# Values of two strided head groups made from neighbouring tokens, and attention steps moved by one slot

## The chip, the cores and the metric

The kernel runs on one core of one Trainium2 chip, in one launch. The time is the device time of one execution in microseconds (us), as the median of three runs. TensorE (PE) multiplies matrices, VectorE (DVE), ScalarE (ACT) and GpSimd (POOL) work on elements, SyncE (SP) issues most DMAs. Each of them takes its instructions in the order in which they were written and stops at one whose input is not there.

## The reference

One decoder block in float32, batch 1, 1024 tokens, width 1024. After a first layer norm, `p = h @ W_in` gives the input of a state-space mixer (SSM), then q, k and v of 12 heads of width 64, and two gates. The heads are three groups of four. Group 0 looks back over 128 neighbouring tokens. In group 1 a query sees only every 4th token and in group 2 every 16th, so these two work on strided subsequences:

```
q, k, v = the slices of p;  q, k = rope_partial(q), rope_partial(k)
for gi, (win, dil) in enumerate(((128, 1), (512, 4), (2048, 16))):
    o_g, lse_g = dilated_window_attention(q[group], k[group], v[group], win, dil)
att = softmax over the three groups of lse, times o
mixed = sigmoid(g_ssm) * GLU(gelu(S5(u))) + sigmoid(g_att) * (att @ W_up)
```

The mixture, memory cross-attention and a feed-forward layer follow, each with a layer norm.

## The kernel before

Every large product is done with three PE products: both factors are split into a rounded high part (made on ACT) and a remainder (made on DVE), and high·high, high·low and low·high are added in PSUM (`mm3`, lines L100 to L102). Weights come through a stream `W`: SP loads a block `wraw`, ACT casts it to `whi` (L136), DVE subtracts to `wlo` (L137). Six split blocks may be held; the stream moves by one block in each *slot*.

A slot is the unit of the order, which is written out by hand: some products, then one attention step, then `slot()`, which moves the weight stream and gives one tick to each generator in `sides`. From 290 to 675 us `qkv_pair` runs for three groups and, in each, for four pairs of token tiles (128 tokens a tile). A pair has six slots: four with the q and k products (12 matmuls of 512 columns each), two with the v products (24 matmuls of 256 columns each). The token tile is the stationary operand (`lhsT`); in groups 1 and 2 it is read with a stride of 4 or 8 tokens (`o.sl`). After the fourth slot `rope` (L906 to L917, DVE) takes q and k out of PSUM and rotates them. After the sixth, L947 adds the bias to v.

The attention of a pair a, b runs beside the products of the next slots. `att_T` (L954) transposes q and k, which needs `rope` to be done. `att_S` multiplies them (L969), takes the masked maximum on DVE (L973, L975) and the exponentials on ACT (L977). `att_PT` (L987) transposes the probabilities. `att_PV` (L995, L996) multiplies them with v, and SP writes the result to `at_dr` (L998). Before, T(a) stands in slot 4 and T(b), S(a) in slot 5 of their own pair (slots are counted from 0); PT(a), S(b) in slot 0, PV(a) in 1, PT(b) in 2 and PV(b) in 3 of the next.

The generator `ssm_side` works through twelve blocks, one in six ticks after four idle ones. Tick 0 of a block is `ssm_pe1` (PE L803, L809; ACT, then DVE L375 fill `dts`), tick 2 is `ssm_pe2` (PE L822, then the DVE chain L826 to L838), tick 5 is `ssm_pe3` (PE L845, L846; DVE `yo`). POOL makes the tables of the next block (L733); `ec` and `es` wait for L837 of this one. With six slots in a pair, `ssm_pe2` always stands in slot 0, behind S(b).

After the last pair come 16 half gates with 32 slots. When the attention's rest and the SSM are done, `launch_merge` starts `merge_side`, whose 23 steps make the input of the next product (L1202 and on), the last of them `yh` and `yl` (L1111, L1112).

Of the kernel before, what the change touches and what calls it, by code (L numbers as in the profile page):

```python
# [10 lines left out]
FT = mybir.dt.float32  # L11
# [8 lines left out]
SEQ = 1024  # L20
D = 1024
NT = SEQ // 128
KB = D // 128
# [35 lines left out]
def block_kernel(ctx, tc, I, out, dbg=None):  # L59
# [33 lines left out]
    def mmbank(shape=(128, 512)):  # L93
        return ps.tile(list(shape), FT, name="mm", tag="mm", bufs=4)
# [6 lines left out]
        pe.matmul(o, lhsT=lh, rhs=rl, start=False, stop=False)  # L101
        pe.matmul(o, lhsT=ll, rhs=rh, start=False, stop=last)  # L102

# [1 line left out]
    class Stream:  # L105
        def __init__(self):
            self.req = []
# [55 lines left out]
    W = Stream()  # L163
# [3 lines left out]
    y_dr = dr.tile([G * 16, 8, 128], FT, name="y_dr")  # L167
    h_dr = dr.tile([NT, 128, D], FT, name="h_dr")
    at_dr = dr.tile([3, SEQ, 264], FT, name="at_dr")
    g_dr = dr.tile([16, 128, SEQ], FT, name="g_dr")  # L170

    for nm, n in (("wxk", 8), ("wu", 6), ("wxv", 8)):
# [4 lines left out]
    for j in range(NG4):  # L177
        W.add(I["wg"][j], 1024, ("wg", j))
        for half in range(2):
            sched4.append(("wg", j, half))  # L180
            n = 2 * j + half
            for key in ab_units[16 * n // (2 * NG4):16 * (n + 1) // (2 * NG4)]:
                sched4.append(key)
                W.add(I[key[0]][key[1]], 1024, key)
    W.nstart = len(W.req)
    for g in range(3):
        for i in range(4):
            W.add(I["wqk"][g, i], 1024)
        for i in range(2):
            W.add(I["wv"][g, i], 1024)  # L190
    for i in range(NG4, 16):
        W.add(I["wg"][i], 1024, ("wg", i))
    for m in range(8):
# [12 lines left out]
        for i in range(4):  # L206
            W.add(I["wff2"][4 * hc + i], 1024)

# [1 line left out]
    stp = con  # L210

    def ln_rstd(sts, e, extra=None):
# [68 lines left out]
                if next(g, "end") == "end":  # L281
                    sides.remove(g)

# [1 line left out]
    kv_c, kvp = open_pool("kv", "left")  # L285
    mem_c, memp = open_pool("memp", "left")
    st_c, stl = open_pool("start", "right")
# [53 lines left out]
        transpose_in(x, hh, hl, t)  # L341
        act.dma_start(h_dr[t], x)

# [1 line left out]
    T = {}  # L345

    def load_bq(g):
# [364 lines left out]
    load_bq(1)  # L712
    par_c, parp = open_pool("par", "right")
    sides.append(params(parp))
# [1 line left out]
    ssm_d = None  # L716

    def start_ssm():
# [164 lines left out]
            ds[b].clear()  # L883
            yield

# [1 line left out]
    att_c, att = open_pool("att", "right")  # L887

    def tok(g, n):
# [29 lines left out]
    def qkv_pair(os_, bias, step):  # L919
        last = os_[0].n == 6  # L920
        ps_ = [mmbank() for _ in os_]
        for i in range(4):
            w = [t.rearrange("p (k c) -> p k c", k=2) for t in W.get(0 if last else i)]
            for o, p in zip(os_, ps_):
                for k in (2 * i, 2 * i + 1):
                    mm3(p, hh[:, k, o.sl], hl[:, k, o.sl], w[0][:, k % 2, :], w[1][:, k % 2, :], k == 0, k == KB - 1)
            if last:
                W.done()
            step(i)
            if i == 3:  # L930
                for o, p in zip(os_, ps_):
                    rope(o, p, bias)
            slot()
        ps_ = [mmbank() for _ in os_]
        for i in range(2):
            w = [t.rearrange("p (k c) -> p k c", k=4) for t in W.get(0 if last else 4 + i)]
            for o, p in zip(os_, ps_):
                for k in range(4 * i, 4 * i + 4):
                    mm3(p[:, :256], hh[:, k, o.sl], hl[:, k, o.sl], w[0][:, k % 4, :], w[1][:, k % 4, :], k == 0,
                        k == KB - 1)  # L940
            if last:
                W.done()
            step(4 + i)
            if i == 1:
                for o, p in zip(os_, ps_):
                    o.v = att.tile([128, 256], FT, name="v", tag="v", bufs=4)
                    dve.tensor_add(o.v, p[:, :256], bias[:, 512:768])  # L947
            slot()

    def att_T(o):  # L950
        p = axbank((128, 4, 128))
# [51 lines left out]
    def steps_old(i):  # L1003
# [7 lines left out]
        elif i == 3:  # L1011
            att_PV(hist[-1], hist[-2])

    for g in range(3):
        if g == 1:
            load_bq(2)
        for n in range(0, 8, 2):
            os_ = [new_tile(g, n), new_tile(g, n + 1)]

            def step(i):  # L1020
                if i < 4:
                    if hist:
                        steps_old(i)
                elif i == 4:
                    att_T(os_[0])
                else:
                    att_T(os_[1])
                    att_S(os_[0], hist[-1] if hist else None)

            qkv_pair(os_, T["bq", g], step)  # L1030
            hist += os_

    def att_tail():
        for i in range(4):
            steps_old(i)
            yield

    sides.insert(0, att_tail())

# [1 line left out]
    state = {"att": att_c, "ssm": ssm_c}  # L1041

    def merge_side():
# [128 lines left out]
    close_pool(state["mg"])  # L1172
    ath, atl, yh, yl = (state[k] for k in ("ath", "atl", "yh", "yl"))

# [1 line left out]
    mx_c, mx = open_pool("mx", "right")  # L1176
    xh = actp.tile([128, KB, SEQ], FR, name="acth", tag="acth")
    xl = actp.tile([128, KB, SEQ], FR, name="actl", tag="actl")
# [41 lines left out]
    close_pool(mx_c)  # L1220
    close_pool(state["yf"])

# [1 line left out]
    nat_c, nat = open_pool("nat", "left")  # L1224
    hn = nat.tile([128, NT, D], FT, name="hn")

# [52 lines left out]

    nat_gemm(xh, xl, evac_mix)  # L1280

# [1 line left out]
    ptp_c, ptp = open_pool("ptp", "right")  # L1283
    ph = ptp.tile([128, 4, SEQ], FR, name="ph")
    pl = ptp.tile([128, 4, SEQ], FR, name="pl")
# [44 lines left out]

    nat_gemm(Cat(ph, xh), Cat(pl, xl), evac_xo)

# [1 line left out]
    fh, fl = ph, pl  # L1334
    for t in range(NT):
        defer(t, lambda t=t: dve.scalar_tensor_tensor(hn[:, t, :], hn[:, t, :], ALPHA, bf2, op0=OP.mult, op1=OP.add))
# [74 lines left out]
def _layout(inputs):  # L1411
# [8 lines left out]
    def natblk(w):  # L1420
        k, n = w.shape
        return c(w.reshape(k // 256, 2, 128, n // 512, 512).transpose(3, 0, 2, 1, 4).reshape(-1, 128, 1024))
# [10 lines left out]
    for k, s in (("ln_in_g", A["ln_in_g"]), ("ln_in_b", A["ln_in_b"]), ("b_mix", A["b_mix_out"][0]),  # L1433
# [13 lines left out]
    o["wu"] = colblk(w_in[:, U:Q])  # L1447
    o["wqk"] = np.stack([natblk(np.concatenate([w_in[:, s + 256 * g:s + 256 * g + 256] for s in (Q, K_)], 1))
                         for g in range(3)])
    o["wv"] = c(np.stack([w_in[:, V + 256 * g:V + 256 * g + 256].reshape(2, 4, 128, 256).transpose(0, 2, 1, 3)  # L1450
                          .reshape(2, 128, 1024) for g in range(3)]))
    o["wg"] = colblk(w_in[:, GS:])
    o["wglu"] = colblk(A["w_glu"][0])
    o["wup"] = colblk(A["w_att_up"][0])
# [39 lines left out]
```

## Time and profile before

| | |
|---|---|
| three runs | 1943.19, 1945.00, 1945.46 us, median 1945.0 |
| span of the profiled execution | 1943.7 us, 1.3 under the median |
| PE busy | 1885.0 us, 97% of the span |
| PE's share of the chain that ended last | 86%, three times 26% of it in L100 to L102 |
| DVE, ACT, POOL busy | 966.7 (50%), 563.7 (29%), 609.0 (31%) us |
| mean granted PE clock | 0.990 |
| DMA | 163.26 MB, mean 84 GB/s |

Only the span is given for the profiled execution; the run's own time around it is not shown, and the timed median stands for it. The span leaves out what lies before its first and after its last instruction. A matmul's duration in the trace is that of its way through the array; what a row of them costs is the distance from one start to the next.

### The profile page before, as it was taken

The page shows a single profiled execution, that of the slowest core. Times are in us where ns is not written, and L with a number is a line of the kernel's source. Part 1 is how long each engine was busy: PE and PEld are TensorE (multiplying, and loading weights), DVE is VectorE, ACT ScalarE, POOL GpSimd, SP SyncE. Part 2 cuts the span into 40 slices and gives each one's busy share as a digit, 9 for nine tenths or more (in the row PEclk, how much of TensorE's full clock was granted, in tenths as well). Part 3 has the DMA queues.
Part 4 walks back from the last instruction along what each step waited for, and adds up shares of the span by engine and source line. Part 5 has one row for each costly group of instructions (what it writes and reads, how often), then busy time and mean ns, then how long its engine had stood idle before and what let it go on. Part 6 is the DMA issues. An engine that isn't in the chain of part 4 may idle for free.

```text
span 1943.7 us, 24170 instructions
## 1 busy us (share of the span) xinstructions
PE 1885.0 (97%) x9400; PEld 1619.6 (83%) x9400; DVE 966.7 (50%) x1678; ACT 563.7 (29%) x998; POOL 609.0 (31%) x782
## 2 busy tenths in 40 slices
PE   7899999999999998999999999999999999999996
PEld 7798788889999976788888888788888888888885
DVE  6526846675666666444556445542323223232328
ACT  4324343433332434322124322412121212213121
POOL 3305687474565335322034004401010100101016
PEclk9999999999999999999999999999999999999998
DMA  6545562130120243333511121111111111011102
GB/s 243 184 122 187 183 198 73 34 99 23 55 67 29 75 136 109 118 117 109 185 44 44 44 76 44 44 65 44 55 54 44 44 44 66 32 55 48 62 21 87
DMA packets 82563, 163.26 MB, mean 84 GB/s; under 512 B 19857, under 2 KB 39441, under 8 KB 82449
## 3 DMA queue, kind: packets, MB, share of 16 engines
q1 hardware_dynamic: 75968, 147.30, 22.8%
q10 hardware_dynamic: 5904, 12.85, 1.7%
q0 software_dynamic: 576, 1.57, 0.3%
q8 instruction: 74, 1.21, 0.3%
q14 instruction: 41, 0.33, 0.1%
HBM read 126.99 MB, written 34.70 MB: 83 GB/s over the span
## 4 chain that ended last, share of the span: by engine, by line
PE 86%; DVE 7%; ACT 2%; issue 2%; POOL 2%; DMA 1%; DVEq 0%; SPq 0%; ACTq 0%; POOLq 0%
PE mm L100 26%; PE mm L102 26%; PE mm L101 26%; PE ax L262 1%; DVE wlo L137 1%; PE ax L996 1%; PE ax L969 1%; PE ax L987 1%; PE ax L822 1%; ACT yh L1111 1%; PE ax L845 1%; PE ax L954 1%; PE ax L809 1%; DVE lnst L237 0%; PE ax L846 0%
## 5 line engine op out<-in xcount | busy, mean ns | idle before, releaser
L100 PE MATMUL mm<-acth,whi 128*128 128x512 f32 (+1 forms) x896 | 348.0, 388 | 4.9 <-ACT abst L611 4.6
L102 PE MATMUL mm<-acth,wlo 128*128 128x512 f32 (+1 forms) x896 | 345.5, 386 | 2.5 <-DVE wlo L137 2.5
L101 PE MATMUL mm<-actl,whi 128*128 128x512 f32 (+1 forms) x896 | 345.4, 386 | 0.3 <-DVE actl L256 0.3
L136 ACT CAST whi<-wraw 128x1024 fp32r<-128x1024 f32 (+1 forms) x169 | 168.4, 996 | 419.5 <-PE mm L102 300.9
L137 DVE TENSOR_TENSOR wlo<-wraw,whi 128x1024 fp32r<-128x1024 f32 (+1 forms) x169 | 213.2, 1263 | 146.9 <-ACT whi L136 144.6
L100 PE MATMUL mm<-whi,acth 128*128 128x512 f32 (+1 forms) x704 | 281.7, 400 | 0.0
L102 PE MATMUL mm<-whi,actl 128*128 128x512 f32 (+1 forms) x704 | 270.7, 384 | 0.0
L101 PE MATMUL mm<-wlo,acth 128*128 128x512 f32 (+1 forms) x704 | 270.4, 384 | 0.0
L1350 POOL TENSOR_TENSOR sg<-sg 128x512 f32<-128x512 f32 x64 | 67.8, 1059 | 574.4 <-ACT sg L1349 574.4
L100 PE MATMUL mm<-whi,ph 128*128 128x512 f32 x576 | 224.3, 389 | 0.0
L102 PE MATMUL mm<-whi,pl 128*128 128x512 f32 x576 | 224.1, 389 | 0.0
L101 PE MATMUL mm<-wlo,ph 128*128 128x512 f32 x576 | 224.1, 389 | 0.0
L100 PEld LDWEIGHTS mm<-acth,whi 128*128 128x128 f32 x896 | 171.1, 191 | 38.4 <-ACT abst L611 5.5
L102 PEld LDWEIGHTS mm<-acth,wlo 128*128 128x128 f32 x896 | 170.6, 190 | 36.4 <-DVE wlo L137 3.0
L101 PEld LDWEIGHTS mm<-actl,whi 128*128 128x128 f32 x896 | 171.1, 191 | 32.6 <-DVE actl L256 0.5
L102 PEld LDWEIGHTS mm<-whi,actl 128*128 128x128 f32 x704 | 168.0, 239 | 15.3
L101 PEld LDWEIGHTS mm<-wlo,acth 128*128 128x128 f32 x704 | 168.6, 239 | 14.2
L100 PEld LDWEIGHTS mm<-whi,acth 128*128 128x128 f32 x704 | 167.5, 238 | 15.4
L1352 DVE TENSOR_TENSOR pl<-sg,ph 128x512 fp32r<-128x512 f32 x64 | 44.3, 692 | 261.8 <-ACT ph L1351 261.8
L1368 DVE TENSOR_TENSOR hn<-hn,mm 128x512 f32<-128x512 f32 x128 | 87.0, 685 | 163.7 <-PE mm L102 163.7
L102 PEld LDWEIGHTS mm<-whi,pl 128*128 128x128 f32 x576 | 108.1, 188 | 22.4
L101 PEld LDWEIGHTS mm<-wlo,ph 128*128 128x128 f32 x576 | 108.1, 188 | 22.4
(322 smaller groups left out, 2882.6 us busy)
## 6 DMA issues: line engine op xcount, KB each, us to landing
wraw<-in_wff_dram SPq DMA_DIRECT2D x64, 512.0 KB
wraw<-in_wg_dram SPq DMA_DIRECT2D x16, 512.0 KB
gl<-g_dr SPq DMA_DIRECT2D x32, 256.0 KB
wraw<-in_wqk_dram SPq DMA_DIRECT2D x12, 512.0 KB
wraw<-in_wglu_dram SPq DMA_DIRECT2D x16, 384.0 KB
g_dr<-abst SPq DMA_DIRECT2D x16, 256.0 KB
a_dr<-abst ACTq DMA_DIRECT2D x16, 256.0 KB
b_dr<-abst ACTq DMA_DIRECT2D x16, 256.0 KB
```

Of the source, the lines that this page charges most:

```text
L100: pe.matmul(o, lhsT=lh, rhs=rh, start=first, stop=False)
L101: pe.matmul(o, lhsT=lh, rhs=rl, start=False, stop=False)
L102: pe.matmul(o, lhsT=ll, rhs=rh, start=False, stop=last)
L136: act.copy(h[:, :n], r[:, :n])
L137: dve.tensor_sub(l[:, :n], r[:, :n], h[:, :n].bitcast(FT))
L262: pe.transpose(p[:, k, :], x[:, (4 * b + k) * 128:(4 * b + k + 1) * 128], ident)
L809: pe.matmul(p[:, g, :], lhsT=xe[:, g].rearrange("p j o -> p (j o)"), rhs=d["cm"][:, g, 0:8, :].rearrange("p j o -> p (j o)"), start=True, ...
L822: pe.matmul(p[:, g, :], lhsT=d["bt"][:, g, :], rhs=d["U"][:, g, :], start=True, stop=True)
L845: pe.matmul(p[:, g, :], lhsT=dts[:, g, :], rhs=d["U"][:, g, :], start=True, stop=False)
L1350: pool.tensor_mul(r, r, r)
L1352: dve.tensor_sub(fl[:, i, s], r, fh[:, i, s].bitcast(FT))
L1368: dve.tensor_add(hn[:, t, cs], hn[:, t, cs], p)
```

## The change

The v products of groups 1 and 2 leave `qkv_pair`. A new `v_pair`, ahead of all groups, makes both groups' values for 128 neighbouring tokens in one product of 512 columns (4 pairs of tiles, 4 slots each, 16 slots without an attention step), adds the bias and writes the rows to a DRAM tensor `v_dr`. `load_v` reads the rows of a strided tile back with one DMA each, in slots 0 and 3. Group 0 keeps its six slots, groups 1 and 2 have four per pair. Their attention steps follow `steps_new`: slot 0 PV(b of the pair before), T(a); slot 1 T(b), S(a); slot 2 PT(a), S(b); slot 3 PV(a), PT(b). One value product is thus left over, also at the end, where the tail has five steps in place of four. The number of slots is 72 as before (16 + 24 + 32), and `ssm_side` is not touched.

```diff
+    v_dr = dr.tile([SEQ, 2, 256], FT, name="v_dr")
...
+    for i in range(4):
+        W.add(I["wv12"][i], 1024)
     for g in range(3):
         for i in range(4):
             W.add(I["wqk"][g, i], 1024)
-        for i in range(2):
-            W.add(I["wv"][g, i], 1024)
+        if g == 0:
+            for i in range(2):
+                W.add(I["wv"][i], 1024)
...
+        if os_[0].g:
+            return
...
+    def v_pair(n, bias):
+        last = n == 6
+        ps_ = [mmbank() for _ in range(2)]
+        for i in range(4):
+            w = [t.rearrange("p (k c) -> p k c", k=2) for t in W.get(0 if last else i)]
+            for t, p in enumerate(ps_):
+                s = slice(128 * (n + t), 128 * (n + t) + 128)
+                for k in (2 * i, 2 * i + 1):
+                    mm3(p, hh[:, k, s], hl[:, k, s], w[0][:, k % 2, :], w[1][:, k % 2, :], k == 0, k == KB - 1)
+            if last:
+                W.done()
+            if i == 3:
+                for t, p in enumerate(ps_):
+                    vt = att.tile([128, 8, 64], FT, name="qk", tag="qk", bufs=2).rearrange("p h d -> p (h d)")
+                    dve.tensor_add(vt, p, bias)
+                    sp.dma_start(v_dr[128 * (n + t):128 * (n + t) + 128].rearrange("q g c -> q (g c)"), vt)
+            slot()
+
+    def load_v(o):
+        o.v = att.tile([128, 256], FT, name="v", tag="v", bufs=4)
+        sp.dma_start(o.v, v_dr[o.sl, o.g - 1, :])
...
+    for n in range(0, 8, 2):
+        v_pair(n, vb[:, 0:2, :].rearrange("p g c -> p (g c)"))
...
+    def steps_new(i):
+        a, b = hist[-2:]
+        if i == 0:
+            if left:
+                att_PV(*left.pop())
+            att_T(a)
+        elif i == 1:
+            att_T(b)
+            att_S(a, hist[-3])
+        elif i == 2:
+            att_PT(a)
+            att_S(b, a)
+        else:
+            att_PV(a, hist[-3])
+            att_PT(b)
+            left.append((b, a))
...
             def step(i):
-                if i < 4:
+                if g:
+                    (steps_new if hist[-1].g else steps_old)(i)
+                    if i in (0, 3):
+                        load_v(os_[i // 3])
+                elif i < 4:
                     if hist:
                         steps_old(i)
...
         for i in range(4):
-            steps_old(i)
+            steps_new(i)
             yield
+        att_PV(*left.pop())
+        yield
```

Because 16 slots now stand ahead of group 0, the ticks of `ssm_side` fall elsewhere in a pair. On PE, before, in the third pair of group 0 (L987 are the transposes PT(a), L969 the scores S(b), L822 is `ssm_pe2`, L100 to L102 the q and k products), the block's second tick is in slot 0:

```order
1685 L987 MATMUL ax<-cst,P 128x128 x8
1686 L969 MATMUL ax<-qkT 128x128 x8
1687 L822 MATMUL ax<-U,bt 128x128 x4
1688 L100 MATMUL mm<-whi,acth 128x512
1689 L101 MATMUL mm<-wlo,acth 128x512
```

And now, in the second pair of group 0, where line numbers differ (L1015 are the transposes PT(b), L826 is `ssm_pe2`):

```order
1815 L1015 MATMUL ax<-cst,P 128x128 x8
1816 L826 MATMUL ax<-U,bt 128x128 x4
1817 L100 MATMUL mm<-whi,acth 128x512
1818 L101 MATMUL mm<-wlo,acth 128x512
1819 L102 MATMUL mm<-whi,actl 128x512
```

`ssm_pe2` moved from slot 0 to slot 2: between it and the products that `rope` takes up there is one slot in place of three. The same holds in all four pairs of group 0, and in the first and last of group 1 and the third of group 2.

On DVE, before, in a pair of group 1 (L973 and L975 are the maxima of S(b), L826 on is the chain of `ssm_pe2`):

```order
472 L973 ISA P,st<-ax,cst 128x256
473 L973 ISA st 128x1
474 L975 TENSOR_SCALAR nm<-st 128x4
475 L826 TENSOR_TENSOR vd<-ax,ec 128x512
476 L827 TENSOR_TENSOR t_4655<-ax,es 64x512
```

And now, in the third pair of group 1 (L839 to L842 end that chain, L1001 are the maxima of S(a)):

```order
610 L839 TENSOR_TENSOR t_5641<-gt,es 64x512
611 L840 TENSOR_TENSOR t_5641<-gt,es 64x512
612 L841 TENSOR_TENSOR gt<-gt,ec 128x512
613 L842 TENSOR_TENSOR gt<-gt,t_5641 128x512
614 L1001 ISA P,st<-ax,cst 128x128
615 L1001 ISA st 128x1
```

A score step stood ahead of the chain; now one stands behind it. This is so in the third pair of group 1, the second of group 2 and the first gate.

## Rows read from the trace of the kernel before

**Rows 1.** Timeline of PE (start, duration, line, operation): ends of four runs.
```profile
290.56 0.39 PE L100 MATMUL mm<-whi,acth 128*128 128x512 f32 x1
...
301.44 0.28 PE L100 MATMUL mm<-whi,acth 128*128 128x256 f32 x1
...
304.20 0.28 PE L102 MATMUL mm<-whi,actl 128*128 128x256 f32 x1
...
433.08 0.40 PE L100 MATMUL mm<-whi,acth 128*128 128x256 f32 x1
...
437.75 0.40 PE L102 MATMUL mm<-whi,actl 128*128 128x256 f32 x1
...
569.90 0.40 PE L100 MATMUL mm<-whi,acth 128*128 128x256 f32 x1
...
574.73 0.40 PE L102 MATMUL mm<-whi,actl 128*128 128x256 f32 x1
```

**Rows 2.** Timeline of PE, starts of slots and attention steps, groups 0 and 1.
```profile
378.86 0.33 PE L995 MATMUL ax<-v,PT 128*128 128x64 f32 x2
...
380.56 0.48 PE L100 MATMUL mm<-whi,acth 128*128 128x512 f32 x1
...
437.99 0.60 PE L954 MATMUL ax<-cst,qk 128*128 128x128 f32 x4
...
439.16 0.62 PE L100 MATMUL mm<-whi,acth 128*128 128x512 f32 x1
...
444.74 0.60 PE L100 MATMUL mm<-whi,acth 128*128 128x512 f32 x1
...
447.77 1.00 PE L996 MATMUL ax<-v,PT 128*128 128x64 f32 x8
448.58 0.60 PE L100 MATMUL mm<-whi,acth 128*128 128x512 f32 x1
```

**Rows 3.** Timeline of DVE in a pair of group 1.
```profile
439.26 0.29 DVE L973 CUSTOM_DVE_ANT_0 P<-ax,cst 128x128 f32<-128x128 f32 x1 [2.56 <-PE ax L969]
...
440.23 0.17 DVE L975 TENSOR_SCALAR nm<-st 128x4 f32<-128x4 f32 x1
...
445.79 0.69 DVE L826 TENSOR_TENSOR vd<-ax,ec 128x512 f32<-128x512 f32 x1
...
452.21 0.69 DVE L838 TENSOR_TENSOR gt<-gt,t 128x512 f32<-128x512 f32 x1
454.20 0.69 DVE L909 TENSOR_TENSOR qk<-mm,bq 128x512 f32<-128x512 f32 x1 [1.31 <-PE mm L102]
...
458.31 0.21 DVE L917 TENSOR_TENSOR qk<-rt 128x64 f32<-128x64 f32 x1
458.45 0.68 DVE L909 TENSOR_TENSOR qk<-mm,bq 128x512 f32<-128x512 f32 x1
...
460.19 0.22 DVE L917 TENSOR_TENSOR qk<-rt 128x64 f32<-128x64 f32 x1
...
468.70 1.97 DVE L375 SCALAR_TENSOR_TENSOR dts<-ax,cst,dts 32x448 f32<-32x448 f32 x4 [7.26 <-ACT dts L813]
```

**Rows 4.** Timeline of POOL, first of six table operations that end at 459.67.
```profile
452.25 1.56 POOL L733 TENSOR_TENSOR ec<-Eac,Ebc 128x512 f32<-128x512 f32 x1 [12.80 <-DVE gt L837]
```

**Rows 5.** Timeline of PE, last pair of group 0; in brackets the wait and its releaser.
```profile
395.99 0.63 PE L954 MATMUL ax<-cst,qk 128*128 128x128 f32 x4 [2.33 <-DVE qk L917]
```

**Rows 6.** The page's costliest groups, a weight block's subtraction: busy, mean ns.
```profile
L137 DVE TENSOR_TENSOR wlo<-wraw,whi 128x1024 fp32r<-128x1024 f32 (+1 forms) x169 | 213.2, 1263 | 146.9 <-ACT whi L136 144.6
```

**Rows 7.** Timeline of ACT, first exponential of a score step of group 1.
```profile
440.48 0.40 ACT L977 ACTIVATE P<-P,nm 128x128 f32<-128x128 f32 x1 [1.28 <-DVE nm L975]
```

**Rows 8.** Waits of PE over the whole span: total, times, longest.
```profile
PE ax L1065 <- POOL am L1085: 9.9, 6, 2.5
...
PE mm L100 <- ACT yh L1111: 0.7, 1, 0.7
```

**Rows 9.** Busy time by engine while those six waits lasted; PEclk is the granted clock.
```profile
720.00:760.00 40.00, 30.53 (x122) 23.37 (x121) 31.05 (x62) 17.00 (x32) 22.68 (x25) 0.91 0.40 128
```

More of the change, by code (lines that the diff above doesn't have):

```diff
@@ L1012, in steps_old @@
             att_PV(hist[-1], hist[-2])
+    vb = att.tile([128, 4, 256], FT, name="P", tag="P", bufs=1)
+    for g in range(2):
+        sp.dma_start(vb[:, g, :], I["b_qkv"][g + 1:g + 2, 512:768].to_broadcast([128, 256]))
+    for n in range(0, 8, 2):
+        v_pair(n, vb[:, 0:2, :].rearrange("p g c -> p (g c)"))
+    left = []
+    def steps_new(i):
[14 more added lines that the diff above has]
+            left.append((b, a))
     for g in range(3):
@@ L1449, in _layout @@
                          for g in range(3)])
-    o["wv"] = c(np.stack([w_in[:, V + 256 * g:V + 256 * g + 256].reshape(2, 4, 128, 256).transpose(0, 2, 1, 3)
-                          .reshape(2, 128, 1024) for g in range(3)]))
+    o["wv"] = c(w_in[:, V:V + 256].reshape(2, 4, 128, 256).transpose(0, 2, 1, 3).reshape(2, 128, 1024))
+    o["wv12"] = natblk(w_in[:, V + 256:V + 768])
     o["wg"] = colblk(w_in[:, GS:])
```

## The prediction

> **What bounds the kernel now.** I read the page first: PE is busy for 97% of the span and carries 86% of the chain that ended last, so only what PE does or waits for can move the time. Then I read PE's timeline in the stretch that the change touches, for the distance between starts. The reader is to see in it that equal products cost different times. In group 0, 48 products of 512 columns take 301.44 − 290.56 = 10.88 us, 0.227 us each, and 23 distances of 256 columns take 2.76 us, 0.120 each. With a strided token tile as the stationary operand, 20 distances of 256 columns take 4.67 us in group 1 (0.2335 each) and 4.83 in group 2 (0.2415 each) [rows 1]. Half the columns cost as much as all of them: the load of the strided operand sets the pace there.
>
> Third, I read the lengths of slots and steps. A q and k slot takes 12 × 0.227 = 2.7 us in group 0 and 447.77 − 444.74 = 3.0 in group 1; a PV takes 1.7 with a previous tile and 0.8 without; T(b) with S(a) takes 1.2 [rows 2]. Fourth came DVE, whose order is that of writing. The chain of the SSM's second step holds it from 445.79 to 452.90, 7.1 us. The rotation of a first tile then takes 454.20 to 458.52, 4.3 us, that of the second 458.45 to 460.41, 2.0 [rows 3]. The difference is POOL: its tables run beside the first and not the second, and they start as the chain ends [rows 4]. PE once waits 2.33 us for a rotation, in the last pair of group 0, where that chain and weight splits made it late [rows 5]. This is the wait to look for.
>
> **The change part by part.** *Products.* Removed are 2 groups × 8 tiles × 24 = 384 products: 192 × 0.2335 + 192 × 0.2415 = 91.2 us. Added are 192 of 512 columns with neighbouring tokens: 192 × 0.227 = 43.6. The sum is −47.6 us, all on PE's path [rows 1].
>
> A rule speaks against this gain. The Trainium skill, "TensorE: Matmul & The Clock Gate", section "LDWEIGHTS (loading the stationary operand)", lets a load's time follow from the number of columns alone, so a stride would cost nothing. By it 384 products would give back 384 × 0.120 − 43.6 = 2.5 us and no more. The trace does not agree with it here: 0.2335 and 0.2415 stand against 0.120 for the same shape.
>
> *The rotation behind the SSM's second step.* With 16 slots ahead of group 0 that step falls into slot 2 in seven pairs. DVE then works 7.1 us on its chain, and the rotation, whose products are done 2.7 to 3.0 us after the step, queues behind it. Its price is 2.0 us free and 4.3 beside POOL's tables; since these start as the chain ends, I take 3.6, nearer the second. T(a) can start 7.1 + 3.6 = 10.7 us after the step. In group 0 PE has work for 2.7 + 1.7 + 24 × 0.120 = 7.3 us (5.6 in the first pair, which has no PV): it waits 3 × 3.4 + 5.1 = 15.3 us, by the two ends 9 to 18. In the first pair of group 1 it has 3.0 + 1.7 + 3.0 = 7.7, in the third of group 2 3.0 + 0.8 + 3.0 + 0.8 = 7.6: two waits of 3.0. In the last pair of group 1 the scores' maxima, four exponentials and a split stand ahead of the chain, 1.1 + 4 × 0.4 + 1.3 = 4.0 us [rows 3, 6, 7]; PE's cover is 3.0 + 0.8 + 3.0 + 1.7 = 8.5 and 0.8 (an estimate, as a PV's) for PT(b), so it waits 10.7 + 4.0 − 9.3 = 5.4. Together 11.4, by the ends 5 to 15.
>
> *Scores behind the same step.* At three places it is in slot 0, ahead of S(a) on DVE. Maxima and first exponential end 7.1 + 1.1 + 0.4 = 8.6 us after it, PE has 3.0 + 1.2 + 3.0 = 7.2, and the four transposes then follow the exponentials: 1.4 + 1.0 = 2.4 each, 7.2 in all. Bounds 3 (the last transposes hidden) to 12 (a rotation still ahead of the chain).
>
> *The first SSM step in slot 2*, three times: the rotation queues behind `dts`, which waits for ACT, 7.26 us in the row, and takes 1.97 [rows 3]. Nothing at best, as the wait lies beside products, 2.0 and some at worst; I take 1.2 each, 3.6 (0 to 7).
>
> *Small waits behind these*: T(b) for the second rotation, score steps for PSUM banks. No row prices them; 0 to 9, and I take 4, as fifteen places at a quarter of a microsecond. *Gone* is the wait of 2.33 [rows 5].
>
> *The clock.* In 720 to 760 us PE waits six times, 9.9 us in all, none over 2.5 [rows 8], and the mean granted clock is 0.91 [rows 9]: 18% of 40 us, 7.2, at 1.2 GHz and not 2.4, which costs 3.6 us of work, a third of what was waited. Now some 40 us are waited, in pieces up to 5.4, but further apart. A third would be 14; I take 11, bounds 0 (clock kept) and 18.
>
> *The tail.* It has five steps, so the merge starts one slot (12 × 0.227 = 2.7 us) later, and the product behind the gates already waits 0.7 us for its last `yh` [rows 8]: +2.7 (0 to 4).
>
> *Transfers and queues.* SP issues 24 DMAs more, ahead of weight loads and of U and y. A value read back in slot 0 or 3 is used a pair, some 20 us, later; weights are two raw and two split blocks ahead. I cost them at nothing; without that cover each late weight block would show as a wait of PE on L137, within the 9 of the small waits.
>
> Sum: −47.6 + 15.3 + 11.4 + 7.2 + 3.6 + 4 − 2.3 + 11 + 2.7 = +5.3 us. The durations come from an execution with a span of 1943.7; the runs' median is 1945.0, and I put the sum on that: 1950. All low ends together give −33, all high ends +34.
>
> **The rivals.** *VectorE catches up* (the other side: faster). If the first rotation takes its free 2.0 us in the seven places because POOL's tables come later or between, waits there fall to 9 + 5, scores to 5, the rest to 2 + 2, and shorter waits cost the clock 5: −47.6 + 14 + 5 + 4 − 2.3 + 5 + 2.7 = −19, 1926. For it speaks the second tile's 2.0, against it that the tables start with the chain's end [rows 4]. It decides from where T(a) waits under 2 us in group 0.
>
> *VectorE becomes the bound.* In a four-slot pair it has two rotations (6), maxima (3), two thirds of the SSM's chains (7) and splits, near 17 us against 20 of PE's work. If POOL also slows the chain and the small waits come to 9: −47.6 + 18 + 15 + 12 + 7 + 9 − 2.3 + 18 + 2.7 = +32; I give this case the middle between that and the forecast, 1968.
>
> *The stride costs nothing in itself*, what the rows show being due to something that stays: −2.5 in place of −47.6 gives 1995. This is the rule named above; the rows speak against it. A sentence on a second one: the Trainium skill, "SBUF — State Buffer", section "SBUF: two separate sides", says that a two-input operation of VectorE and one of GpSimd exclude each other for a whole instruction, by which all seven rotations would take the 4.3 us and the sum would be 5 us higher, 1955; the trace agrees with it in the one row pair shown.
>
> **How the numbers follow.** The forecast, that waits and clock eat the gain, has a chance of 0.50 and a range of its own of 1940 to 1960; VectorE catching up 0.28, 1912 to 1941; VectorE the bound 0.20, 1960 to 1979; the stride rule 0.02. A measurement of this kernel tells about 0.2%, 3.9 us, from no change. Of the forecast's half, 0.02 lies below 1941.1 and 0.17 within 3.9 us; of the second case 0.26 below and 0.02 within. That is faster 0.28, same 0.19, slower 0.53. The range for 8 in 10 cuts a tenth at each side: 1928 to 1968.
>
> **What would show it.** Right: 192 products of 512 columns at 0.227 apart ahead of group 0, none of 256 with a strided tile; T waiting for the rotation's last line 3 to 5 us in each pair of group 0, and 5 or more in the last pair of group 1; transposes of P waiting for exponentials in the third pair of group 1 and the second of group 2; a granted clock under 1.00 between 340 and 700 us. Wrong: waits of PE in those stretches of under 25 us in sum (then it is faster), or new waits on L137 or on a DMA, which I put at nothing.

## The result, and the profile after

The changed kernel takes 1987.6 us (median of four runs, 1986.4 to 1989.2) against 1944.8 for the kernel before on the same chip: 42.9 us more, a ratio of 1.0217 with a 95% interval of 1.0204 to 1.0230. The direction of the forecast was right, though its 5 us were hardly more than the 3.9 that it could tell from no change. Its size, 1950 with a range of 1928 to 1968, was not. The profiled execution took 1986.4 us, with a span of 1984.6.

These are lines of the page after: busy time (share of the span) and instructions, the clock that PE was granted in 40 equal slices, in tenths, and the chain that ended last, by engine.

```profile
PE 1864.5 (94%) x9208; PEld 1583.3 (80%) x9208; DVE 972.5 (49%) x1670; ACT 562.9 (28%) x998; POOL 606.0 (31%) x782
...
PEclk9999999898998998899999999999999999999998
...
PE 76%; DVE 14%; issue 3%; ACT 3%; POOL 2%; DMA 2%; SPq 0%; DVEq 0%; ACTq 0%; POOLq 0%
```

PE is busy for 20.5 us less than before, yet the span is 40.9 us longer, so PE now stands still for 61 us more. DVE's share of the chain has doubled from 7 to 14%, although it works only 5.8 us more. The slices with an 8 (each is 49.6 us long) lie behind the value slots: two in group 0, one where group 1 ends and group 2 begins, two in the merge; the mean granted clock is 0.969 and was 0.990. The next view lists PE's waits over the whole span of after: who was waited for, total, times, longest. After, L982 is the transpose T, L1124 that of the merge, L1015 that of the probabilities, L1170 the last `yh`, L850 the SSM's third step. The single line below the view is the wait for weights in the kernel before.

```profile
PE ax L982 <- DVE qk L921: 43.3, 8, 11.1
PE ax L1124 <- POOL am L1144: 14.6, 6, 4.5
PE mm L102 <- DVE wlo L137: 8.5, 6, 1.8
PE ax L1015 <- ACT P L1005: 8.2, 3, 3.2
...
PE mm L100 <- ACT yh L1170: 4.8, 1, 4.8
PE ax L850 <- DVE gt L842: 4.5, 2, 3.7
```

```profile
PE mm L102 <- DVE wlo L137: 8.3, 6, 1.8
```

The first row answers to the single wait of [rows 5], the second and the one on `yh` to [rows 8]. Waits for weights (L137) are where they were, 8.5 against 8.3 us, and no wait on a DMA is new: the trip of the values through DRAM costs nothing that shows. The timeline of PE after shows the products and the waits one by one (start, duration, line, operation; in brackets the idle time and who ended it).

```profile
290.63 0.39 PE L101 MATMUL mm<-wlo,acth 128*128 128x512 f32 x1
...
294.48 0.39 PE L100 MATMUL mm<-whi,acth 128*128 128x512 f32 x1
...
373.45 1.09 PE L982 MATMUL ax<-cst,qk 128*128 128x128 f32 x4 [11.10 <-DVE qk L921]
...
443.05 1.09 PE L982 MATMUL ax<-cst,qk 128*128 128x128 f32 x4 [4.33 <-DVE qk L921]
...
481.56 1.09 PE L982 MATMUL ax<-cst,qk 128*128 128x128 f32 x4 [7.58 <-DVE qk L921]
...
600.39 1.09 PE L982 MATMUL ax<-cst,qk 128*128 128x128 f32 x4 [7.70 <-DVE qk L921]
...
601.72 0.63 PE L101 MATMUL mm<-wlo,acth 128*128 128x512 f32 x1
...
604.70 0.63 PE L102 MATMUL mm<-whi,actl 128*128 128x512 f32 x1
...
674.41 1.02 PE L982 MATMUL ax<-cst,qk 128*128 128x128 f32 x4 [3.70 <-DVE qk L921]
```

Two things are to be seen. In the new value slots 17 distances take 294.48 − 290.63 = 3.85 us, 0.227 each, as in group 0 [rows 1]. And the waits stand at the seven places that the prediction named (the two that are not shown are 4.3 in the second pair of group 0 and 4.1 in the first of group 1), but each is longer than it said. Behind them products come 0.426 us apart for some microseconds (2.98 us for seven distances from 601.72), not 0.227. This is the lower of the clock's two levels, 1.2 GHz: the granted clock of that stretch, the number after the five engines, is 0.50.

```profile
601.72:604.70 2.98, 2.98 (x8) 2.34 (x7) 2.30 (x3) 0.38 (x1) 1.50 (x2) 0.50 0.14 47
```

What PE waits for at 443.05, in the third pair of group 0, stands in the timeline of DVE: the SSM chain, then the rotation of the first tile.

```profile
431.40 0.69 DVE L830 TENSOR_TENSOR vd<-ax,ec 128x512 f32<-128x512 f32 x1 [2.20 <-issue]
...
434.25 1.37 DVE L836 TENSOR_TENSOR_SCAN gt<-r,vd 128x128 f32<-128x128 f32 x4
...
437.81 0.69 DVE L842 TENSOR_TENSOR gt<-gt,t 128x512 f32<-128x512 f32 x1
438.42 0.68 DVE L913 TENSOR_TENSOR qk<-mm,bq 128x512 f32<-128x512 f32 x1
439.14 0.42 DVE L918 TENSOR_TENSOR rt<-qk,rope_c 128x128 f32<-128x128 f32 x1
439.49 1.13 DVE L919 TENSOR_TENSOR rt<-qk,rope_s 128x128 f32<-128x128 f32 x1
440.65 1.24 DVE L920 TENSOR_TENSOR qk<-rt 128x64 f32<-128x64 f32 x1
441.82 1.08 DVE L921 TENSOR_TENSOR qk<-rt 128x64 f32<-128x64 f32 x1
442.82 0.68 DVE L913 TENSOR_TENSOR qk<-mm,bq 128x512 f32<-128x512 f32 x1
```

The chain takes 7.1 us, as in [rows 3]; the rotation follows it at once and takes 442.82 − 438.42 = 4.4 us, from its first start to that of the second tile's. POOL's tables start when the chain lets go of `ec`, in this row of POOL's timeline, as in [rows 4]:

```profile
437.85 1.56 POOL L737 TENSOR_TENSOR ec<-Eac,Ebc 128x512 f32<-128x512 f32 x1 [8.67 <-DVE gt L841]
```

In the first pair the chain itself is slow. DVE's timeline there, in which L836 are the four scans:

```profile
356.82 0.69 DVE L830 TENSOR_TENSOR vd<-ax,ec 128x512 f32<-128x512 f32 x1 [2.26 <-PE ax L826]
...
359.70 4.46 DVE L836 TENSOR_TENSOR_SCAN gt<-r,vd 128x128 f32<-128x128 f32 x4
...
368.22 0.69 DVE L842 TENSOR_TENSOR gt<-gt,t 128x512 f32<-128x512 f32 x1
```

It takes 368.91 − 356.82 = 12.1 us; the same scans take 1.37 us in the next pairs. POOL makes the tables `bm` and `cmx` from 358.06 to 366.92 beside it. A block's six slots take 21.5 us where they are value slots (308.11 to 329.61 between two second steps), and POOL, with its waits, needs 24.4 us from one block's `ec` to the next (317.67 to 342.11), so its tables fall behind into the chain.

The last new loss lies behind the gates' start, where the prediction had one small term. A row of DVE's timeline in the merge after, then two that stand there in the merge before:

```profile
748.32 1.56 DVE L137 TENSOR_TENSOR wlo<-wraw,whi 128x768 fp32r<-128x768 f32 x1 [1.99 <-ACT whi L136]
```

```profile
719.69 0.96 DVE L1083 TENSOR_TENSOR am<-am,mw 128x768 f32<-128x768 f32 x1
720.57 0.95 DVE L137 TENSOR_TENSOR wlo<-wraw,whi 128x768 fp32r<-128x768 f32 x1
```

A weight block is split every fourth slot and a merge tile takes two. After, the split falls into the slot that makes a tile's weights, ahead of them, and DVE stands still 2 us for ACT's copy; before, it fell into the other slot, where the copy was long done. With a split a tile takes 10.3 us after (744.72 to 755.02 between the merge's transposes), without one 8.5.

### The profile page after: what moved, and what is told of

The parts are those of the page before. It is cut to its first block, busy times and chain, and to the rows that moved or that the text cites. A ratio compares the mean times of both kernels' runs of the same rounds, so it can differ in the third digit from the quotient of the medians.

```text
span 1984.6 us, 23846 instructions
## 1 busy us (share of the span) xinstructions
PE 1864.5 (94%) x9208; PEld 1583.3 (80%) x9208; DVE 972.5 (49%) x1670; ACT 562.9 (28%) x998; POOL 606.0 (31%) x782
## 4 chain that ended last, share of the span: by engine, by line
PE 76%; DVE 14%; issue 3%; ACT 3%; POOL 2%; DMA 2%; SPq 0%; DVEq 0%; ACTq 0%; POOLq 0%
PE mm L100 23%; PE mm L102 23%; PE mm L101 23%; DVE wlo L137 2%; PE ax L266 1%; DVE gt L836 1%; PE ax L997 1%; ACT whi L136 1%; PE ax L982 1%; PE ax L849 1%; PE ax L1015 1%; PE ax L850 1%; PE ax L1024 1%; DVE lnst L241 0%; DVE vd L833 0%
## 5 line engine op out<-in xcount | busy, mean ns | idle before, releaser
L100 PE MATMUL mm<-acth,whi 128*128 128x512 f32 (+1 forms) x896 | 349.5, 390 | 5.2 <-ACT abst L615 5.0
L102 PE MATMUL mm<-acth,wlo 128*128 128x512 f32 (+1 forms) x896 | 345.8, 386 | 2.5 <-DVE wlo L137 2.5
L137 DVE TENSOR_TENSOR wlo<-wraw,whi 128x1024 fp32r<-128x1024 f32 (+1 forms) x169 | 214.2, 1269 | 182.3 <-ACT whi L136 179.8
L100 PE MATMUL mm<-whi,acth 128*128 128x512 f32 (+1 forms) x640 | 261.7, 409 | 0.0
L101 PE MATMUL mm<-wlo,acth 128*128 128x512 f32 (+1 forms) x640 | 250.8, 392 | 0.0
L102 PE MATMUL mm<-whi,actl 128*128 128x512 f32 (+1 forms) x640 | 250.4, 391 | 0.0
L100 PE MATMUL mm<-whi,ph 128*128 128x512 f32 x576 | 224.3, 389 | 0.0
L102 PE MATMUL mm<-whi,pl 128*128 128x512 f32 x576 | 224.1, 389 | 0.0
L100 PEld LDWEIGHTS mm<-acth,whi 128*128 128x128 f32 x896 | 171.5, 191 | 39.1 <-ACT abst L615 5.8
L102 PEld LDWEIGHTS mm<-acth,wlo 128*128 128x128 f32 x896 | 171.0, 191 | 36.9 <-DVE wlo L137 3.0
L102 PEld LDWEIGHTS mm<-whi,actl 128*128 128x128 f32 x640 | 140.4, 219 | 19.5
L100 PEld LDWEIGHTS mm<-whi,acth 128*128 128x128 f32 x640 | 140.9, 220 | 18.6 <-issue 0.4
L101 PEld LDWEIGHTS mm<-wlo,acth 128*128 128x128 f32 x640 | 141.2, 221 | 17.9
L102 PEld LDWEIGHTS mm<-whi,pl 128*128 128x128 f32 x576 | 108.1, 188 | 22.5
```

Of the source, the lines that this page charges most:

```text
L100: pe.matmul(o, lhsT=lh, rhs=rh, start=first, stop=False)
L137: dve.tensor_sub(l[:, :n], r[:, :n], h[:, :n].bitcast(FT))
```

## The experiments

Times are medians, and ratios are to runs of the kernel before on the same chip (1944.5 to 1945.1 us). The runs were spread over chips, so a difference between two of them is good to about 0.6 us and their own spread.

**The merge, moved alone in the kernel before.** `b_merge1`, and `b_merge2` with two such steps:

```diff
         for i in range(4):
             steps_old(i)
             yield
+        yield
```

> The kernel before with one empty step at the end of the attention's tail, so that the merge starts one slot later and nothing else moves. Theory P (phase): a weight split (copy on ACT, subtraction on DVE) then falls into the slots in which the merge's weights are made, ahead of them on DVE, which stands still some 2 us for ACT's copy, as in the kernel after; every second tile of the merge takes 10.3 us and not 8.4, PE waits 14 to 15 us at the merge's transposes and not 9.9, and 3 to 5 at the last yh and not 0.7: +10 to +18 us. Theory D (delay, the prediction's term): the merge is late by one slot of 2.7 us and by no more: +1 to +4 us.

> The kernel before with two empty steps at the end of the attention's tail: the merge starts two slots later. Theory P (phase): the split falls again beside the other half of a merge tile, as in the kernel before; DVE does not stand still for ACT's copy, tiles take 8.2 us as before, and only the last products ahead of the GLU wait longer: +0 to +7 us, less than with one empty step. Theory D (delay): two slots of 2.7 us, +4 to +6 us, more than with one.

One slot costs 1958.3 − 1945.1 = 13.1 us (ratio 1.0066, 1.0051 to 1.0081), two slots 7.1 us (1.0038, 1.0025 to 1.0051). PE's waits, with one step and then with two (lines are shifted by one and two):

```profile
PE ax L1066 <- POOL am L1086: 14.8, 5, 4.5
...
PE mm L100 <- ACT yh L1112: 4.2, 1, 4.2
```

```profile
PE ax L1067 <- POOL am L1087: 10.7, 7, 2.6
...
PE mm L100 <- ACT yh L1113: 5.4, 1, 5.4
```

One slot later costs more than two: the phase decides (how the merge's slots lie to the weight splits), as theory P said. Two slots bring the tiles' waits back to 10.7 us, and what is left is the plain delay at the last `yh`. P put this run at 0 to 7, so its end was a little low.

**The merge one slot sooner in the kernel after**, `a_tail4`:

```diff
         for i in range(4):
             steps_new(i)
+            if i == 3:
+                att_PV(*left.pop())
             yield
-        att_PV(*left.pop())
-        yield
```

> The kernel after with the last PV of the attention's tail put into its fourth step, so that the merge starts one slot sooner, as far behind the gates' first slot as in the kernel before. Theory P (phase): 10 to 18 us faster than the kernel after, so 25 to 33 us slower than the kernel before; PE's waits at the merge's transposes fall from 14.6 to some 10 us, that at the last yh from 4.8 to under 1. Theory D (delay): 1 to 4 us faster than the kernel after, 39 to 42 us slower than before.

1976.5 us (1.0160, 1.0145 to 1.0175): 11.2 us of the change's loss go with one PV moved by one slot. The waits, beside those of after above:

```profile
PE ax L982 <- DVE qk L921: 43.5, 8, 11.2
PE ax L1124 <- POOL am L1144: 9.9, 6, 2.6
...
PE mm L100 <- ACT yh L1170: 0.9, 1, 0.9
```

The merge is as before the change again, and the waits for the rotation stay. This kernel (the four-step tail below) is the base of the following ones.

**The stride alone**, `b_vnear`:

```diff
-                    mm3(p[:, :256], hh[:, k, o.sl], hl[:, k, o.sl], w[0][:, k % 4, :], w[1][:, k % 4, :], k == 0,
+                    mm3(p[:, :256], hh[:, k, 128 * o.n:128 * o.n + 128], hl[:, k, 128 * o.n:128 * o.n + 128], w[0][:, k % 4, :], w[1][:, k % 4, :], k == 0,
```

> The kernel before, in which the value products of groups 1 and 2 take 128 neighbouring tokens as their stationary tile and not those of the group (the values then belong to other tokens); every step stays where it is. Theory S (the stride sets the pace): 384 products fall from 0.2335 and 0.2415 us to 0.120 apart, 192 x 0.1135 + 192 x 0.1215 = 45 us of PE, of which waits for the rotation of the first tile take some back, as PE's cover for it falls by 2.7 us in eight pairs: 33 to 45 us faster. Rival: the pace belongs to something else in these slots (the evictions, the weights' arrival) and stays: within 3 us.

1910.7 us, 34.4 less (0.9821, 0.9807 to 0.9836). Two rows of its PE timeline in group 1, 20 distances apart:

```profile
425.62 0.28 PE L100 MATMUL mm<-whi,acth 128*128 128x256 f32 x1
...
428.02 0.28 PE L102 MATMUL mm<-whi,actl 128*128 128x256 f32 x1
```

The stride sets the pace: with neighbouring tokens the same products of the same shape come 2.40 / 20 = 0.120 us apart, where [rows 1] have 0.2335, and the kernel, which computes other tokens' values, saves 34 us. Of the 10.7 that are missing to 45.1, 5.5 are waits for the rotation, 7.8 us against 2.3, because the value slots that covered it are shorter. PE's busy time fell by 41.2 us (1885.0 to 1843.8), so some 4 of the remaining 5 are in products that took longer elsewhere; the granted clock is 0.988, before 0.990.

**The moved steps alone**, `b_ssm0`:

```diff
-SSM_LAG = 4
+SSM_LAG = 0
```

> The kernel before with the SSM's steps begun at once (a lag of 0 slots, not 4), its products unchanged: the second step then stands in slot 2 of every pair of all three groups, as it does after the change in group 0, and the SSM ends four slots sooner, which nothing waits for. Theory W with the sizes measured after the change: 20 to 28 us of waits for the rotation in group 0, 0 to 2 in each of the eight pairs behind it, whose strided value slot covers 5.6 us and not 2.9, and 10 to 15 of clock: +30 to +55 us. With the sizes of the prediction (3.4 each, 5.1 in the first): 15 of waits and 5 of clock, +15 to +25. Rival V (what costs are the new value slots, not the moved steps): within 6 us.

1996.2 us, 51.2 more (1.0264, 1.0248 to 1.0280), with all products as before. PE's timeline, the transposes of the first, second and fourth pair of group 0 (4.35 in the third):

```profile
321.89 1.12 PE L954 MATMUL ax<-cst,qk 128*128 128x128 f32 x4 [11.27 <-DVE qk L917]
...
355.94 0.63 PE L954 MATMUL ax<-cst,qk 128*128 128x128 f32 x4 [4.36 <-DVE qk L917]
...
430.30 1.09 PE L954 MATMUL ax<-cst,qk 128*128 128x128 f32 x4 [6.45 <-DVE qk L917]
```

The first three waits are those of after to 0.2 us and the fourth is 1.1 shorter, in a kernel without its value slots. The place of the chain makes them, and one number in the order costs 2.6%. That the first agrees so well is luck in part. The chain is slow in that pair too, 304.61 to 317.43, 12.8 us, but here it is that of the first block, and POOL has just begun the next block's tables (`bm` and `cmx`, 307.00 to 316.16). The four scans in DVE's timeline there:

```profile
307.49 4.34 DVE L832 TENSOR_TENSOR_SCAN gt<-r,vd 128x128 f32<-128x128 f32 x4
```

**The chain at other places**, `a4_ssm3` and `a4_ssm1`: the four-step tail with a lag of 3, and of 1.

```diff
-SSM_LAG = 4
+SSM_LAG = 1
```

> The kernel after with the last PV in the tail's fourth step (1976.5 us) and the SSM's steps begun one slot sooner (a lag of 3 slots, not 4): its second step then stands in slot 1 of every pair of group 0, one slot of 2.7 us further from the rotation, and in slots 1 and 3 of the pairs of groups 1 and 2. Theory W (the chain stands too near the rotation): the 43.5 us that transposes wait for the rotation fall under 15, the granted clock rises from 0.970 towards 0.985, and 35 to 60 us go: 1917 to 1942, below the kernel before. Rival B (VectorE has too much to do in a pair, wherever it stands): the waits only move, to the scores and the second rotation, and under 15 us go: above 1961.

> The kernel after with the last PV in the tail's fourth step (1976.5 us) and the SSM's steps begun three slots sooner (a lag of 1): its second step stands in slot 5 of every pair of group 0, behind the rotations and the first tile's maxima, and in slots 1 and 3 of the pairs of groups 1 and 2. Theory W (place decides): no transpose waits more than 1 us for a rotation in group 0, the first pair's 8.7 of the lag of 3 goes too; 10 to 20 us faster than that kernel's 1952.8: 1933 to 1943. Rival B (VectorE has too much to do): the second tile's maxima behind the chain and the transposes of P wait in place of it: 1948 or more.

The lag of 3 gives 1952.8 us (1.0035, 1.0023 to 1.0047), 23.7 less than the four-step tail. The waits for the rotation fell from 43.5 to 13.8 us, under 15 as W said, but 8.7 of them stayed in the first pair, where the chain takes 12.0 us (354.27 to 366.28), and 10.3 us in seven new places came at the scores, which wait for ACT's copies of the transposed probabilities. The time lies between the two theories. The lag of 1 gives 1936.5 (0.9957, 0.9942 to 0.9972), 40.0 less than with a lag of 4 and 8.1 less than the kernel before, as W said. PE's waits in it:

```profile
PE ax L1124 <- POOL am L1144: 10.7, 6, 3.4
PE ax L850 <- DVE gt L842: 9.4, 3, 3.8
...
PE ax L982 <- DVE qk L921: 0.7, 1, 0.7
```

DVE does the same work with both lags. Behind the rotations the chain makes PE wait 0.7 us for them, ahead of them 43.5. B, that VectorE has too much to do, falls. No run looks for a better lag in the kernel before, so what the change is worth between the best orders of both kernels stays open.

**POOL's tables**, `a4_notab`, which leaves them out from the second block on, then two ways to move them:

```diff
-                for _ in range(3):
-                    next(gens[b + 1])
+                ds[b + 1].update({q: ds[b][q] for q in ("bm", "cm", "ec", "es")})
...
-            if b < 11:
-                for _ in gens[b + 1]:
-                    pass
```

> The kernel after with the last PV in the tail's fourth step (1976.5 us), without the SSM's tables from the second block on (POOL makes none beside the attention, and every block takes those of the first). Theory N (POOL's tables stretch the rotation from 2.0 to 4.4 us and the chain in the value slots from 7.1 to 12.1): the seven waits for the rotation fall by 2.4 us each and the first by 5 more, from 43.5 to 18 to 25 us, that of the third SSM step goes, the clock gives 8 to 15 us back: 27 to 40 us faster, 1936 to 1950. Rival C (the chain's own 7.1 us set the waits, the tables only fill them): under 12 us faster.

1928.0 us (0.9915, 0.9896 to 0.9934), 48.5 less than the four-step tail and more than N's 40. The waits for the rotation fell from 43.5 to 16.9 us: that of the first pair from 11.2 to 3.4, which shows that POOL's tables make the slow chain there, the other six by 2.9 to 4.3 each. In all PE is idle for 32.6 us less and busy for 18.5 less with the same products; for the clock N had put 8 to 15. `a4_eclate` writes `ec` and `es` two ticks later:

```diff
-            if b < 11:
-                for _ in gens[b + 1]:
-                    pass
             yield
             yield
+            if b < 11:
+                for _ in gens[b + 1]:
+                    pass
             yield
```

> The kernel after with the last PV in the tail's fourth step (1976.5 us), and the second half of the SSM's tables (ec, es) written two slots later, so that POOL does not start them as the chain ends and the first rotation runs beside no table. Theory N: that rotation takes 2.0 us and not 4.4, six or seven waits fall by 2.4 us each, the clock gives 4 to 8 back: 15 to 26 us faster, 1950 to 1961. Rival M (POOL's work is as long wherever it stands, and meets the maxima, the splits or the next block's chain): within 6 us of 1976.5, with the waits at the transposes of P or at the third SSM step in place of those for the rotation.

1977.0 us (1.0167, 1.0152 to 1.0182): no change, and the waits for the rotation are 43.7 us in place of 43.5. The time is the one that M gave, but not for M's reason: both theories looked at the wrong thing. Nothing else stands in POOL's queue there, so its order was the same, and the traces show the same sequence of instructions on PE, DVE, ACT and POOL in both kernels; when the tables start is set by DVE's release of `ec`. `a4_ecwait` therefore makes POOL wait for data (`qk_last` holds the rotated tiles; the diff is against the one above):

```diff
...
             if b < 11:
+                if qk_last:
+                    tq = stb.tile([128, 8], FT, name="tq", tag="tq", bufs=1)
+                    pool.tensor_copy(tq, qk_last[-1][:, 7, 0:8])
                 for _ in gens[b + 1]:
                     pass
```

> The kernel after with the last PV in the tail's fourth step (1976.5 us), where POOL, ahead of the second half of each block's tables (ec, es), copies 8 columns of the second rotated tile, and so cannot start these tables before both rotations are done. (Writing them later alone moved nothing: POOL's queue holds nothing else, and only the buffers' release held them.) Theory N (POOL's tables stretch the first rotation): its last four lines take 1.1 and not 4.0 us, each of the seven waits falls by 2.4 to 2.9 us, 43.5 to some 24, and the clock gives 5 to 10 back: 20 to 30 us faster, 1946 to 1957. Rival M (the tables are as long wherever they run and meet the maxima, the splits and the next chain): under 8 us faster.

1948.6 us (1.0018, 1.0007 to 1.0029), 27.9 less than the four-step tail, as N said. In DVE's timeline of this kernel the rotation behind the chain is free of POOL:

```profile
434.22 0.68 DVE L919 TENSOR_TENSOR qk<-mm,bq 128x512 f32<-128x512 f32 x1
434.94 0.29 DVE L924 TENSOR_TENSOR rt<-qk,rope_c 128x128 f32<-128x128 f32 x1
...
435.61 0.22 DVE L927 TENSOR_TENSOR qk<-rt 128x64 f32<-128x64 f32 x1
```

and POOL's, in which the copy holds the tables back:

```profile
437.27 0.19 POOL L887 COPY tq<-qk 128x8 f32<-128x8 f32 x1 [11.24 <-DVE qk L926]
437.42 1.06 POOL L737 TENSOR_TENSOR ec<-Eac,Ebc 128x512 f32<-128x512 f32 x1
```

1.6 us (434.22 to 435.83) in place of 4.4. The line that adds the bias to the products in PSUM takes 0.68 either way; the four with both inputs in SBUF take 0.9 (from 434.94) alone, and beside POOL 3.8 (439.14 to 442.90). The Trainium skill, "SBUF — State Buffer", section "SBUF: two separate sides", says just this: an operation of VectorE with two SBUF inputs and one of GpSimd that reads SBUF lock each other out for a whole instruction. These rows agree. With the lag of 1 the same copy, `a4_ssm1_ecwait`, has little left to free:

> The lag of 1 together with POOL's copy of the rotated tile ahead of ec and es. Where the chain stands behind the rotations (slots 5 and 3), the copy holds nothing up and changes nothing; in slot 1 of groups 1 and 2 it frees the rotation behind the chain. Theory N with W: 0 to 6 us faster than the lag of 1 alone. Rival: the copy delays the tables into the next block's chain and the kernel is slower than with the lag of 1 alone.

1934.6 us (0.9952, 0.9938 to 0.9967), 1.9 less than without the copy, which the intervals don't tell apart; the rival's slowing did not come.

**The clock**, `a4_warm`:

```diff
+    WARM = {(0, 0): 40, (0, 2): 16, (0, 4): 16, (0, 6): 28, (1, 0): 14, (1, 6): 28, (2, 4): 13}
     def att_T(o):
+        n = WARM.get((o.g, o.n), 0)
+        if n:
+            p = axbank((128, 512))
+            for _ in range(n):
+                pe.matmul(p, lhsT=hh[:, 0, 0:128], rhs=hh[:, 0, 0:512], start=True, stop=True)
```

> The kernel after with the last PV in the tail's fourth step (1976.5 us), in which PE does throwaway products of 512 columns (13 to 40, of some 0.227 us) ahead of the seven transposes that wait for a rotation, so that it works through most of each wait; nothing reads them. Theory K (what the waits cost beyond themselves is the clock: PE's products behind them run at 1.2 GHz): the granted clock rises from 0.970 to 0.985 or more and 12 to 25 us go, 1951 to 1964, with the waits' rows nearly filled. With the prediction's size of the clock (a third of what was waited, 11 us for all waits): 5 to 10 us go. Rival: the slow products have another cause, and the added ones cost or change nothing: within 4 us, or slower.

1959.1 us (1.0076, 1.0059 to 1.0092): 155 useless products, 35.2 us of work at 0.227, make the four-step tail 17.4 us faster. The granted clock rose from 0.970 to 0.984. PE is busy for 20.1 us more (1863.8 to 1883.9), not 35.2, so all its other work took 15.1 less. The waits for the rotation that PE still had are

```profile
PE ax L989 <- DVE qk L921: 7.4, 8, 1.3
```

So 36.1 us of idle time were filled, and each had cost another 17.4 / 36.1 = 0.48 us, most of it in products at the lower clock.

**The value slots**, `a5_late3` and `a4_ssm1_notab`: the lag of 1, with the third SSM step of three blocks a slot later, and without tables as above.

```diff
             yield
+            if b < 3:
+                yield
             ssm_pe3(b, ds[b])
             ds[b].clear()
-            yield
+            if b >= 3:
+                yield
```

> The lag of 1 (1936.5 us) with the third SSM step of the first three blocks one value slot later, in the slot of the next block's first step. Theory T (in the value slots of 2.7 us six slots are shorter than what POOL's tables and DVE's chain need): the three waits for the chain there (3.5, 2.1, 3.8) fall by up to 2.7 each, 7.5 in all, and the clock gives 2 to 5 back: 1923 to 1930. Rival Q (the delay only moves on): the next block's second step waits for dts instead, and the time stays within 4 us.

> The lag of 1 (1936.5 us) without the SSM's tables from the second block on (every block takes those of the first). Theory T: the 9.4 us of waits for the chain in the value slots vanish, the rest of the waits stays within 3 us, the clock gives 4 to 8 back: 1916 to 1926. Rival (once the chain stands behind the rotations, POOL's tables cost nothing): above 1932.

The later step gives 1934.2 us (0.9940, 0.9924 to 0.9957): Q's time, not T's. The waits for the chain fell from 9.4 to 3.1, but 4.2 us came at the next block's first step, for POOL's `cmx`, and 3.3 at transposes of P. The wait for `dts` that Q named stayed at 3.0. Without tables it is 1909.7 (0.9815, 0.9798 to 0.9832), 26.8 less and below T's 1916. Its waits at the transposes of P, and for the chain:

```profile
PE ax L1011 <- ACT P L1001: 7.2, 4, 4.2
...
PE ax L850 <- DVE gt L842: 0.4, 1, 0.4
```

What holds PE in the value slots and just behind them is POOL's time for the tables, which moving PE's steps does not shorten. The versions that compute everything and beat both kernels are those with the lag of 1, 8 to 10 us under the kernel before.

## Why the prediction was wrong in size

*Products, −47.6.* Right: 0.227 after, none strided for the values, and the stride alone brings the products from 0.2335 to 0.120 and gives 34.4 us where 45.1 was reckoned. That a load's time follows from the number of columns alone (the Trainium skill, "TensorE: Matmul & The Clock Gate", section "LDWEIGHTS (loading the stationary operand)") does not hold for these strided tiles by that run.

*The rotation behind the second step, 15.3 + 11.4 = 26.7.* Right in all seven places and in kind, too small in each: 43.3 less the 0.5 of a place that had another cause. This is the step that failed first. The rotation was taken at 3.6 us; it was 4.4 every time, close to the 4.3 in the row of before. I went below the measured 4.3 although the tables start as the chain ends; they do, and so they meet the whole of it. The rule on the shared port that stood beside the sum was right, but the 5 us that it adds are a small part of what was missing. In the first pair the chain was taken at 7.1 and was 12.1 (5 of the 11.1 us), since POOL's tables, late from the value slots, run beside the scans, which no row of before showed. In the last pair of group 0 two weight splits, the second behind a late copy, stood ahead of the chain (7.6 against 3.4), and in the last pair of group 1 the split that I had put ahead of it came 1.5 us later than reckoned (7.7 against 5.4).

*The scores behind the same step, 7.2*: 8.2, at the three places named. *`dts`, 3.6*: 0.5. *Small waits, 4*: 4.5, all at the third SSM step in and just behind the value slots, where I looked for none: the size is right by luck. *Gone, −2.3, and transfers, 0*: right.

*The clock, 11.* Too small. A third of what is waited was read from [rows 8] and [rows 9]; behind these longer waits it was 0.48 us for each, 17.4 for the seven filled ones alone. PE's busy time gives the whole: it fell by 20.5 us where the products are worth −47.6, so the rest of PE's work took 27.1 us longer, for 61.4 us more of idle time. The price is not a constant: in `b_ssm0`, with all products as before, it was 12.0 us (1885.0 to 1897.0) for 38.2 us more of idle time, about the third that I took.

*The tail, 2.7.* Failed as a mechanism: 11.2 us. I priced the delay of a slot, and it was the phase against the weight splits, which the rows of DVE in the merge before could have shown, had I read the order of split and tile there.

With the measured terms the sum is −47.6 − 2.3 + 43.3 + 8.2 + 4.5 + 11.2 = +17.3; to 42.9 there are 25.6, close to the 27.1 by which PE's other work was slower (some 2 of which are in the tail's 11.2); 17.4 are shown by a run to go when the waits are filled, and the other 8 are put down to the clock by that count alone.

Of the rivals, the stride that costs nothing came nearest in time (1995), by luck: its cause falls by `b_vnear`. VectorE as the bound (1968) had the condition that POOL slows the chain, which held in the first pair only, and its cause falls too: with the same work in another order the waits vanish. VectorE catching up needed a first rotation at its free price. `a4_ecwait` makes that, with the merge's slot put right, and takes 1948.6 us, not 1926, because the chain's 7.1 us still stand ahead of the rotation. Two numbers were added wrongly, without weight for the outcome: all high ends together give +33, not +34, and the middle between +32 and the forecast is 1964, not 1968.

## What to carry to other kernels

A change that adds or takes whole slots shifts every other generator against the one that it edits: list where each long DVE chain and each weight split now stands, and price the phase, not the delay. Price an operation beside another engine by the row that shows it there, and a wait of PE at more than its length once the clock falls behind it (here 1.3 to 1.5 times). To move work on an engine with an empty queue, change what it waits for; where its lines are written does nothing.

## What was not expected of the hardware

Useless products in PE's waits made a kernel 17.4 us faster. Four scans of 128x128 took 1.37 us with no table of POOL beside them and 4.46 with. One slot of delay in the merge cost 13.1 us and two cost 7.1.
